# Issuing a third load ahead of the entry barrier, and a small row of the second load on another engine's queue

## The chip, the cores and the metric

One core of a Trainium2 chip. The metric is the device time of one execution in microseconds (us). The profile of an execution is shorter by about 1.3 us, since its span runs from the first to the last instruction. A run is called slow when it is over 1.5% above the fastest of the same kernel; verdicts and ratios use fast runs alone.

## The reference

```python
def reference(x):                      # x: (16, 1024, 512) float32
    x_scaled = x / 2.0
    x_max = np.max(x_scaled, axis=-1, keepdims=True)
    exp_x = np.exp(x_scaled - x_max)
    return exp_x / np.sum(exp_x, axis=-1, keepdims=True)
```

It is a softmax over the last axis: 16384 rows of 512 numbers, 33.55 MB in and as much out.

## The kernel before

The rows are loaded in ten tiles of 3, 5, 15, 15, ... rows per partition. ScalarE takes the exponential of each row and its sum, VectorE the reciprocals and the products, SyncE issues the stores. Loads 0 and 1 are issued ahead of the barrier with which the program starts; GpSimd issues the last two loads, which reuse space. (The maximum is not subtracted unless the row sums fall out of range; that path is not taken here.)

```python
TILES = [(3, 0), (5, 3), (15, 8), (15, 23), ...]      # rows per partition, place in the arena
SPREAD = 1

def load(eng, t):
    r = tiles[t][1]
    parts = [(0, P, 0, r)]
    if t == SPREAD:      # second load: four rows, then its last row on 126 and on 2 partitions
        parts = [(0, P, 0, r - 1), (0, 126, r - 1, r), (126, P, r - 1, r)]
    for p, q, lo, hi in parts:
        eng.dma_start(out=sb(t)[p:q, lo:hi], in_=dram(xf, t)[p:q, lo:hi]).then_inc(ld[t], 16)

def early():                      # put in ahead of the entry barrier
    load(nc.sync, 0)
    load(nc.scalar, 1)

def loads():                      # behind it
    for t in range(2, min(LATE)):
        load(nc.scalar, t)
# ... cut: for t in range(len(tiles)): TensorE waits for ld[t] and lets ScalarE go on;
#     GpSimd waits for s_exp >= starts.index(TURN), TURN = 83 rows, and for the stores whose
#     space loads 8 and 9 reuse, and then issues these
```

## Time and profile before

| | |
|---|---|
| time | 159.91 us (159.89 to 159.91) |
| span of the profile | 158.7 us |
| DMA | 423 GB/s over the span |
| ScalarE, VectorE busy | 51%, 46% |
| last multiply ends, last store lands | 143.6 us, 158.7 us |

How to read it: no engine is busy for much more than half of the span, while the 16 DMA engines are full. What sets the end is how fast 67.11 MB go through them, and the last store only waits for its turn. The lines are in the prediction below. There and below, an issuing engine's ring is the list of packets that its transfers have waiting on one DMA engine.

### The profile page before, as it was taken

The numbers are of one execution on the slowest core, as the hardware profiler recorded it, in microseconds if no ns is written. First come the engines' busy times: TensorE is split into PE (matmuls) and PEld (weight loads), VectorE is DVE, ScalarE is ACT, GpSimd is POOL, SyncE is SP. The second block draws the span as 40 slices with busy tenths as digits, with TensorE's granted clock in tenths as the row PEclk, the third lists the DMA queues.
The fourth block names the chain that finished last, engine by engine and source line by source line (L and its number), as shares of the span: only waits on it lengthen the run. The fifth ranks groups of instructions, "written<-read, shape, count | busy, mean of one in ns | idle before, by whom it ended". The sixth has DMA issues, their size and how long they took to land. (4 is left out here: it accounts for less than half of the span.)

```text
span 158.7 us, 657 instructions
## 1 busy us (share of the span) xinstructions
PE 0.2 (0%) x2; PEld 0.1 (0%) x2; DVE 73.2 (46%) x27; ACT 80.8 (51%) x257; POOL 2.2 (1%) x8
## 2 busy tenths in 40 slices
PE   0000000000000000000000000000000000000000
PEld 0000000000000000000000000000000000000000
DVE  0047001992981990059500991008932981992000
ACT  0590598697498008940399001991597009940000
POOL 0000000000000000000000300000000000010000
DMA  7999998989999999999999999999999999999995
GB/s 271 382 496 396 463 437 324 480 382 485 410 457 410 457 410 449 418 449 418 441 426 441 426 434 434 426 441 426 441 418 449 418 449 410 457 403 465 403 457 256
DMA packets 3024, 67.11 MB, mean 423 GB/s; under 512 B 336, under 2 KB 336, under 8 KB 720
## 3 DMA queue, kind: packets, MB, share of 16 engines
q1 hardware_dynamic: 1584, 34.34, 50.4%
q10 hardware_dynamic: 1152, 24.90, 37.1%
q0 software_dynamic: 288, 7.86, 11.5%
HBM read 33.55 MB, written 33.55 MB: 423 GB/s over the span
## 5 line engine op out<-in xcount | busy, mean ns | idle before, releaser
L271 ACT ACTIVATE arena<-arena x125 | 76.8, 615 | 54.1 <-ACTq L140 54.1
L169 DVE TENSOR_TENSOR arena<-arena,recip 128x7680 f32<-128x7680 f32 (+2 forms) x12 | 70.2, 5847 | 0.4
L166 DVE RECIPROCAL recip<-stats 128x15 f32<-128x15 f32 (+2 forms) x12 | 2.7, 224 | 70.4 <-ACT arena L271 61.4
L271 ACT ACTIVATION_READ_ACCUMULATOR arena<-arena x125 | 23.4, 187 | 0.0
L200 ACT ACT_TABLE_LOAD x1 | 1.3, 1283 | 5.7 <-issue 5.7
L119 POOL DMA_DIRECT2D arena<-in_x_dram x2 | 1.3, 638 | 84.9 <-ACT arena L271 84.9
L204 ACT ACTIVATE arena<-arena 128x512 f32<-128x512 f32 x3 | 1.9, 619 | 0.0
L180 POOL TENSOR_SCALAR inside<-stats 128x128 f32<-128x128 f32 x1 | 0.6, 630 | 51.7 <-ACT arena L271 51.7
L204 ACT ACTIVATION_READ_ACCUMULATOR arena<-arena 128x1 f32 x3 | 0.6, 188 | 0.0
L196 PE MATMUL total<-ones,count 128*1 128x1 f32 x2 | 0.2, 164 | 143.9 <-DVE inside L184 143.9
L184 DVE SCALAR_TENSOR_TENSOR inside<-inside,stats 128x128 f32<-128x128 f32 x1 | 0.3, 282 | 0.0
L188 DVE TENSOR_SCALAR flag<-total 1x1 int32<-1x1 f32 x1 | 0.1, 146 | 0.3 <-PE total L196 0.3
L196 PEld LDWEIGHTS total<-ones,count 128*1 128x1 f32 x2 | 0.1, 80 | 143.9 <-DVE inside L184 143.9
L175 POOL MEMSET ones<- 128x1 f32 x1 | 0.1, 98 | 2.2 <-POOLq L37 2.2
L306 POOL MEMSET const-bfloat16-1.0<- 128x1 bf16 x1 | 0.1, 108 | 0.0
L306 POOL MEMSET const-uint8-127<- 128x1 uint8 x1 | 0.1, 108 | 0.0
L306 POOL MEMSET const-float32-0.0<- 128x1 f32 x1 | 0.1, 104 | 0.2 <-issue 0.2
L306 POOL MEMSET const-float32-1.0<- 128x1 f32 x1 | 0.1, 104 | 0.0
L184 DVE DVE_READ_ACCUMULATOR inside<-inside,stats 128x1 f32 x1 | 0.1, 80 | 0.0
## 6 DMA issues: line engine op xcount, KB each, us to landing
out_dram<-arena SPq DMA_DIRECT2D x8, 3840.0 KB, 26.2
arena<-in_x_dram ACTq DMA_DIRECT2D x6, 3840.0 KB, 46.7
arena<-in_x_dram POOLq DMA_DIRECT2D x2, 3840.0 KB, 33.6
out_dram<-arena SPq DMA_DIRECT2D x1, 1280.0 KB, 22.9
arena<-in_x_dram ACTq DMA_DIRECT2D x1, 1024.0 KB
arena<-in_x_dram SPq DMA_DIRECT2D x1, 768.0 KB, 5.6
out_dram<-arena SPq DMA_DIRECT2D x1, 768.0 KB, 14.6
arena<-in_x_dram ACTq DMA_DIRECT2D x1, 252.0 KB
```

The costliest lines, as they stand in the source:

```text
L119: eng.dma_start(out=sb(t)[p:q, lo:hi], in_=dram(xf, t)[p:q, lo:hi]).then_inc(ld[t], 16)
L166: nc.vector.reciprocal(out=recip[:, b : b + c], in_=stats[:, b : b + c])._wait_ge(s_exp, ks[-1] + 1).then_inc(s_rec, 1)
L169: nc.vector.tensor_mul(out=arena[:, a : a + c], in0=arena[:, a : a + c], in1=recip[:, b : b + c].unsqueeze(2).to_broadcast([P, c, D]),)._w ...
L175: nc.gpsimd.memset(ones[:, :], 1.0).then_inc(s_ones, 1)
L180: nc.gpsimd.tensor_scalar(out=inside[:, :], in0=stats[:, :], scalar1=LO, scalar2=HI, op0=Alu.max, op1=Alu.min,)._wait_ge(s_exp, len(sizes) ...
L184: nc.vector.scalar_tensor_tensor(out=inside[:, :], in0=inside[:, :], scalar=1.0, in1=stats[:, :], op0=Alu.mult, op1=Alu.is_equal, accum_ou ...
L188: nc.vector.tensor_scalar(out=flag[:, :], in0=total[:, :], scalar1=float(N), scalar2=None, op0=Alu.is_ge,)._wait_ge(s_tot, 1).then_inc(s_f ...
L196: nc.tensor.matmul(total[:, :], lhsT=count[:, :], rhs=ones[:, :], start=True, stop=True)._wait_ge(s_cnt, 2).then_inc(s_tot, 1)
L200: nc.scalar.preload_act_table(Exp)
L204: ins = nc.scalar.activation(out=arena[:, b], in_=arena[:, b], func=Exp, scale=0.5, accum_out=stats[:, b : b + 1],)
L271: ins = nc.scalar.activation(out=data, in_=data, func=Exp, scale=0.5, accum_out=stats[:, r : n_rows - E + 1 + r][:, bass.ds(now, 1)],)
L306: nc = _bacc.Bacc("TRN2", target_bir_lowering=False, num_devices=1)
```

## The change

Its intent is to have the third load in the queue sooner, to free ScalarE of two issues at the start, and to let the small row of the second load travel on a second queue.

```diff
-            eng.dma_start(
+            (eng if q - p == P else nc.sync).dma_start(
                 out=sb(t)[p:q, lo:hi], in_=dram(xf, t)[p:q, lo:hi]
             ).then_inc(ld[t], 16)
 ...
         load(nc.scalar, 1)
+        load(nc.scalar, 2)
 ...
-        for t in range(2, min(LATE)):
+        for t in range(3, min(LATE)):
             load(nc.scalar, t)
```

> **What bounds the kernel now.** I read the page first (busy shares, slices, chain), then the DMA view, then windows along the span, then the timeline of the first 20 us, where the change lies.
>
> ```profile
> span 158.7 us, 657 instructions
> ...
> PE 0.2 (0%) x2; PEld 0.1 (0%) x2; DVE 73.2 (46%) x27; ACT 80.8 (51%) x257; POOL 2.2 (1%) x8
> ...
> DMA  7999998989999999999999999999999999999995
> GB/s 271 382 496 396 463 437 324 480 382 485 410 457 410 457 410 449 418 449 418 441 426 441 426 434 434 426 441 426 441 418 449 418 449 410 457 403 465 403 457 256
> DMA packets 3024, 67.11 MB, mean 423 GB/s; under 512 B 336, under 2 KB 336, under 8 KB 720
> ```
>
> No engine is busy for more than 51% of the span, while the 16 DMA engines stand at 8 or 9 tenths in every slice but the first and the last. 67.11 MB must move (33.55 in, 33.55 out), so the bound is the transfer of bytes. The chain of waits ends at 144.3 us, 14 us before the span does, and carries only 6% of it: the rest of the end is a store in flight, which the chain does not show.
>
> ```profile
> 134.67 2.83 DVE arena L169
> ...
> 140.81 2.83 DVE arena L169
> 143.63 0.22 DVE inside L184 x2
> ...
> 144.12 0.15 DVE flag L188
> ```
>
> The last store is issued when the multiply of 140.81 ends (143.64). The semaphore updates in the trace say that the store before it lands at 148.7 to 149.6 us, so the last store stands in the ring some 5 us before its turn. That 5 us is the slack of compute at the end. The packet records give the sum: 2048 packets of 30720 bytes take 1.138 us each (2330.6 us), 256 of 6144 bytes 0.234 (59.9), 128 of 8192 bytes 0.309 (39.6), 128 of 2048 bytes 0.084 (10.8), 128 of 10240 bytes 0.385 (49.3): 2490.2 us of engine time, over 16 engines 155.6 us. First data moves at 1.0 us, last at 158.18, that is 157.2 us. So only 1.5 us in the whole kernel is not packets at their usual pace, and a change of the issue order has to get its gain out of this 1.5 us.
>
> Where it lies, by packets that took longer than usual, as a mean over 16 engines: 0.25 us in the first load's first packets, 0.13 in the second load's, 0.37 in the first packet of the third load on every engine (1.5 instead of 1.14 us, all starting 6.4 to 7.0), 0.39 around 24 to 27 us where the first store gives way to the second. The start in the timeline:
>
> ```profile
> 0.00 0.38 SPq L119 DMA_DIRECT2D arena<-in_x_dram  x1
> 0.13 5.51 ACTq L119 DMA_DIRECT2D arena<-in_x_dram  x9
> ...
> 5.67 1.28 ACT L200 ACT_TABLE_LOAD   x1 [5.67 <-issue]
> 6.96 0.63 ACT L204 ACTIVATE arena<-arena 128x512 f32<-128x512 f32 x1
> ...
> 8.82 0.61 ACT L271 ACTIVATE arena<-arena  x1
> ...
> 10.94 4.48 SPq L137 DMA_DIRECT2D out_dram<-arena  x2
> ...
> 17.71 0.63 ACT L271 ACTIVATE arena<-arena  x1 [5.73 <-ACTq L140]
> ```
>
> ScalarE issues nine loads in 5.51 us, loads its table, works the first load from 6.96, the second (five rows) from 8.82 and then waits for the third until 17.71. The single instructions: second load 0.13 to 0.52, its 126-partition part 0.56 to 1.22, the 2-partition part 1.25 to 1.49, the barrier, then the third load at 2.66. Yet the third load's first packet moves at 6.45, 3.4 us after its issue ended, because the rings are full of the first two loads until then.
>
> ```profile
> 1.00:2.00 1.00, 0.00 (x0) 0.00 (x0) 0.00 (x0) 0.00 (x0) 0.00 (x0) 1.00 0.92 283
> 2.00:3.00 1.00, 0.00 (x0) 0.00 (x0) 0.00 (x0) 0.00 (x0) 0.10 (x1) 1.00 0.96 391
> 3.00:4.00 1.00, 0.00 (x0) 0.00 (x0) 0.00 (x0) 0.00 (x0) 0.00 (x0) 1.00 0.98 401
> 4.00:5.00 1.00, 0.00 (x0) 0.00 (x0) 0.00 (x0) 0.00 (x0) 0.00 (x0) 1.00 1.11 449
> ```
>
> The last two columns are DMA share and GB/s: from 2 us on the engines are full (0.96 and more). The barrier, which holds the third load until 2.66, starves nothing.
>
> **What the Trainium skill says.** "DMA: Bandwidth & Descriptors", section "Issuing engines are not separate DMA queues": transfers from ScalarE and SyncE run on the same 16 engines, and issuing from several saves only the sequencer's issue time. The trace agrees: 423 GB/s over everything. Same page, "Queues, rings and completion order": the two issuers own one ring each on every engine, and the engine goes round robin between rings packet by packet. The trace agrees: the first store, 768 KB, which alone would need 1.9 us (128 x 0.234 / 16), takes 14.6 us to landing, because its eight packets per engine alternate with 30 KB packets of the loads (starts about 1.37 us apart, and 1.138 + 0.234 is 1.372). Same page, "Why a DMA increments its semaphore by 16 and not by 1": the number of engines is the largest divisor up to 16 of the slowest dimension, so the 126-partition part runs on 14 engines (9 packets each) and the 2-partition part on 2 (the lowest numbered); the packet records carry no engine, so the trace shows this at most by its 0.67 us issue, longest of the nine.
>
> **The change part by part.** Bytes, packets and the engines they run on stay the same; two things move.
>
> (a) The third load's issue (0.36 us) comes ahead of the barrier, from 2.66 to about 0.56 on ScalarE. It is in the ring some 2 us earlier, but the ring has older work until 6 us: worth 0 by itself.
>
> (b) The two small parts (0.67 + 0.24 us of issue) go from ScalarE to SyncE. ScalarE is through its early issues at about 0.13 + 0.39 + 0.04 + 0.36 = 0.92 instead of 1.49; SyncE at 0.38 + 0.04 + 0.67 + 0.03 + 0.24 = 1.36 instead of 0.38. The barrier waits for the later of the two, so it falls some 0.1 to 0.2 us earlier. Behind it five loads of about 0.52 us remain: 2.5 + 2.6 = 5.1 instead of 5.64. The table load starts near 5.15, the first activation near 6.45 instead of 6.96, the first store is issued near 10.4 instead of 10.94. All of it beside a full DMA: 0 at the end.
>
> (c) The order on the rings changes, and this is the largest effect to be seen. The small row's 2 KB packets now stand on SyncE's ring behind the first load, beside ScalarE's ring of second and third load. When the first load ends (4.3 to 4.9 us), half of the second load is out (of 8 packets per engine some 4 are left). Alternating, SyncE's ring gives its completion and four small packets for ScalarE's four remaining 8 KB packets and completion. From there each small packet waits behind a 30 KB packet of the third load. Five are left and a completion: on engines with nine, 6.3 + 0.37 + 6 x 1.14 + 5 x 0.08 = 13.9 us; on the two engines that also have the tenth, two rounds more, 16.3. Before, the second load was known complete at 7.9 us. So it lands at 14 to 17 us, 6 to 9 later.
>
> (d) What this delays: ScalarE's five rows of the second load run from about 16.5 to 19.6 (5 x 0.615), the third load's fifteen (9.23 us) from 19.6 to 28.9 instead of 17.71 to 27.05. The fourth load lands at 28.9 in either kernel (activation at 29.26), so ScalarE has caught up there. VectorE's multiply of the second load ends near 19.7 + 0.2 + 2.83 = 22.8, its store is issued there instead of 15.09. But in the kernel before that store stood in the ring until 25.9 us, behind the first store. The first store now starts behind the small row, near 14, and needs 8 x 1.37 = 11 us, so until 25: the second store is still in time or nearly. The third store goes from 35.5 to about 37.4; loads take the turns left free.
>
> Sum on the path that sets the end: bytes 0, issue 0, idle DMA 0, and from the 1.5 us of slow packets a piece that may change: 0.37 us for the third load's first packet and 0.39 at the hand-over between stores. I take -0.1 for both together.
>
> **The rivals.**
> 1. Gain of the full 0.37 us: with the third load in the ring early, its first read is hidden under the mixed packets. For it: 30 KB packets that alternate with 6 KB stores show no such excess. Against it: the third load had been in the ring for 3.4 us before it started slow, so a late issue was not the cause. It would make 159.5.
> 2. The late second load carries on: late stores, late reuse of buffers, a starved DMA later. For it: compute is in order, and the second load comes before the third on ScalarE and VectorE. Against it: ScalarE has 1.5 to 11 us of waits ahead of every later load, the loads that reuse buffers are issued at 87.7 while the first three stores have landed at 57.3 already, and 5 us of slack remain at the end. If it did go through whole, it would be 160.5 to 162.
> 3. The small row does not get caught: its packets are through before the third load's start, because the ring favours SyncE. Then the second load lands near 7.5, everything runs 0.5 us earlier, and the end is the same, 159.8 to 159.9.
> 4. Small packets between 30 KB reads slow the reads: 128 packets, each with 0.3 us more on one engine, would be 2.4 us over the 16; the pairs of 6 and 8 KB show about 0.02 us more per packet, which is 0.2 us at most. It would make 160.1.
>
> **Range and chances.** Base 159.91, three runs within 0.02, less 0.1: 159.8. Rival 1 gives the low side, 159.3 with some gain at the store hand-over; rivals 2 and 4 the high side, 160.3. Over 2% is 3.2 us: for faster, twice the 1.5 us there is, so 0.01; for slower, 3 us of newly idle DMA, which only rival 2 in a shape I can't see would bring: 0.02.
>
> **What would show it.** Right: the second load's first activation at 14 to 17 us instead of 8.82 and the table load near 5.15 (steps b, c); ScalarE without a wait between second and third load, and at the fourth load back to about 29.3 (d); second store issued near 23; DMA at 9 tenths throughout and a last store still issued 3 us or more before its predecessor lands. Wrong: a slice with the DMA under 8 tenths between 10 and 150 us (rival 2), the second load complete before 9 us (rival 3), 30 KB packets over 1.3 us while small ones remain (rival 4), or the end moved by more than 0.5 us with none of these.

## The result and the profile after

The changed kernel takes 160.97 us (160.4 to 161.65, six runs), the kernel before in the same rounds 159.92 (159.89 to 160.07). The ratio is 1.0059, with a 95% interval of 1.0032 to 1.0086. A ratio here is the mean time of one kernel's fast runs over that of the other's fast runs of the same rounds, so it is not quite the ratio of the medians. The change is "within 2%", as foreseen, but it costs some 0.6%, the runs scatter over 1.2 us where those of before scatter over 0.2, and 160.97 lies outside the predicted range.

The page after, the rows that answer to those of before (busy times; DMA share and GB/s in 40 slices):

```profile
span 159.6 us, 657 instructions
...
PE 0.2 (0%) x2; PEld 0.1 (0%) x2; DVE 73.2 (46%) x27; ACT 80.5 (50%) x257; POOL 2.2 (1%) x8
...
DMA  7999999999899999999999999999999989898986
GB/s 277 465 391 401 450 425 375 444 467 436 377 485 393 470 393 470 416 446 408 439 446 416 400 423 393 470 400 470 393 470 393 477 385 477 385 485 385 477 385 262
DMA packets 3024, 67.11 MB, mean 420 GB/s; under 512 B 336, under 2 KB 336, under 8 KB 720
```

Work, packets and bytes are the same; only the mean rate has fallen, from 423 to 420 GB/s, with the DMA engines as full as before. So nothing starves: the same packets take longer.

The timeline of the start, after (start, length, engine, line, operation; in brackets the idle time before it):

```profile
0.00 1.17 SPq L119 DMA_DIRECT2D arena<-in_x_dram  x3
0.12 4.63 ACTq L119 DMA_DIRECT2D arena<-in_x_dram  x7
...
4.78 1.28 ACT L201 ACT_TABLE_LOAD   x1 [4.78 <-issue]
6.08 0.63 ACT L205 ACTIVATE arena<-arena 128x512 f32<-128x512 f32 x1
...
10.05 28.22 SPq L137 DMA_DIRECT2D out_dram<-arena  x3
17.09 0.63 ACT L272 ACTIVATE arena<-arena  x1 [9.07 <-ACTq L140]
...
20.51 2.82 DVE L170 TENSOR_TENSOR arena<-arena,recip 128x2560 f32<-128x2560 f32 x1
...
29.76 8.16 DVE L170 TENSOR_TENSOR arena<-arena,recip 128x7680 f32<-128x7680 f32 x1
```

ScalarE's issues end 0.9 us earlier, and the first load is worked on 0.9 us earlier (6.08, before 6.96). The second load's work starts at 17.09 where it started at 8.82; from there on ScalarE runs without a wait through the third load. All this is as foreseen. The chain that ended last:

```profile
138.39 2.82 DVE arena L170
141.21 0.22 DVE inside L185 x2
...
141.71 0.15 DVE flag L189
```

The last multiply ends at 141.21, 2.4 us *earlier* than before (143.63), and still the last store lands later: its sixteen completions come at 157.73 to 158.66 before and at 158.23 to 159.59 after, four of the latter behind 159.1. Compute has gained and the DMA has lost.

Windows of the two kernels show where (start:end, length, busy time of five engines, clock, DMA share, GB/s). Before:

```profile
20.00:60.00 40.00, 0.00 (x0) 0.00 (x0) 25.23 (x6) 25.71 (x85) 0.00 (x0) 1.00 1.00 426
60.00:100.00 40.00, 0.00 (x0) 0.00 (x0) 16.82 (x4) 20.03 (x65) 1.27 (x2) 1.00 1.01 435
100.00:150.00 50.00, 0.19 (x2) 0.09 (x2) 26.22 (x13) 26.43 (x86) 0.63 (x1) 1.00 1.00 433
```

After:

```profile
20.00:60.00 40.00, 0.00 (x0) 0.00 (x0) 28.24 (x8) 30.24 (x99) 0.00 (x0) 1.00 1.00 431
60.00:100.00 40.00, 0.00 (x0) 0.00 (x0) 16.82 (x4) 18.76 (x63) 1.27 (x2) 1.00 0.99 420
100.00:150.00 50.00, 0.19 (x2) 0.09 (x2) 26.22 (x13) 25.38 (x83) 0.63 (x1) 1.00 1.00 433
```

Between 60 and 100 us the rate is 420 GB/s instead of 435, at a DMA share of 0.99 (between 20 and 60 us it is a little higher than before, 431 instead of 426). Nothing in the source points at that stretch: the change is in the first 3 us.

For the rest I use the trace's packet records. Each packet has a usual duration by its size (30720 bytes 1.138 us, 8192 bytes 0.309, 6144 bytes 0.234, 2048 bytes 0.084); "excess" is what the packets took beyond it, summed and divided by the 16 engines. Excess by the time at which packets start, in us:

| profile of | 0-20 | 20-40 | 40-100 | from 100 | sum | last store lands: first, median, last engine | run's time |
|---|---|---|---|---|---|---|---|
| before | 0.86 | 0.39 | 0.01 | 0.07 | 1.33 | 157.7, 158.0, 158.7 | 160.05 |
| after | 1.00 | 0.12 | 0.81 | 0.02 | 1.95 | 158.2, 158.5, 159.6 | 160.98 |

The mean engine loses 0.62 us more, and the slowest engine 0.93 us more.

### The profile page after: what moved, and what is told of

Its sections match the earlier page's. It is cut to its first block, busy times and chain, and to the rows that moved or that the text cites. A ratio compares the mean times of both kernels' runs of the same rounds, so it can differ in the third digit from the quotient of the medians.

```text
span 159.6 us, 657 instructions
## 1 busy us (share of the span) xinstructions
PE 0.2 (0%) x2; PEld 0.1 (0%) x2; DVE 73.2 (46%) x27; ACT 80.5 (50%) x257; POOL 2.2 (1%) x8
```

## The experiments

Theories at the start: **A**, the order on the rings costs the time (2 KB packets of the small row alternate with 30 KB packets of the third load, and the second load is late because of it); **B**, the early issue of the third load itself does. All sixteen experiments gave correct results. The kernel before ran beside every job, 44 times in all. Ten of those were slow (166.8 to 168.7 us), so slow runs belong to no variant in particular; the fast ones lay between 159.75 and 160.13. e1 to e4 are one job; f1, its reference, f4 and f5 the next; then g1 to g4 and h1 to h4.

**e1: the third load early, the small row left on ScalarE.** From the changed kernel:

```diff
-            (eng if q - p == P else nc.sync).dma_start(
+            eng.dma_start(
```

> Only the third load's early issue; the small row stays on ScalarE's ring, ahead of the third load. Theory A (the order on the rings costs the time: small packets alternating with the third load's 30 KB packets, and the second load late because of it): packets come in the order of the kernel before, so 159.9 +- 0.2 us, second load complete near 7.9 us. Theory B (the early issue of the third load itself costs): 160.4 to 161.6.

Measured: 159.94 us, ratio 0.9999 (0.9986 to 1.0013), second load complete at 7.91. B falls: the early issue is worth nothing and costs nothing.

**e2: the small row on SyncE, the third load behind the barrier.** From the changed kernel: `load(nc.scalar, 2)` taken out of `early()` and put back into `loads()`.

> Only the small row on SyncE's ring; the third load issued behind the barrier, near 2.3 us, still before the rings reach it at 6.3. Theory A: as the changed kernel, 160.4 to 161.6 us with scatter over 0.5, second load complete near 16.7. Theory B: 159.9 +- 0.2.

Measured: 160.69 us (160.48 to 161.02), ratio 1.0053 (1.0040 to 1.0066), second load complete at 16.89. This half of the change carries all of its cost.

**e3: the small row issued ahead of the first load.**

```diff
-        load(nc.sync, 0)
         load(nc.scalar, 1)
+        load(nc.sync, 0)
         load(nc.scalar, 2)
```

> The changed kernel with the small row issued ahead of the first load on SyncE, so that it alternates with 8 KB packets and is through before the third load starts. Theory A: second load complete near 8 us, 159.9 +- 0.3 us, small scatter. Theory B, or SyncE's issue of a 14-engine transfer as the cost: 160.4 to 161.6.

Measured: four of seven runs slow (164.0 to 164.5); the fast ones 159.95, 160.19 and 160.28, ratio 1.0020 (1.0002 to 1.0039). The design was poor: with the small row in front, it was now the first load that met the third, and its completions came at 14.2 to 16.8 us instead of 5.6. Under A the cost should have moved, not vanished; the run tells little.

**e4: the second load's work late, the loads' packets as before.** From the kernel before:

```diff
         for t in range(len(tiles)):
+            if t == SPREAD:
+                nc.tensor.wait_ge(ld[t + 1], 16)
             nc.tensor.wait_ge(ld[t], 48 if t == SPREAD else 16).then_inc(...)
```

> The kernel before, in which the work on the second load is held until the third has landed (near 17 us); the loads' packets unchanged. Splits theory A: A1 (lateness of the second load's work and of the stores behind it, which shifts how stores and loads meet on the engines later) 160.4 to 161.6 us with scatter; A2 (small packets among 30 KB packets and the engines put out of step by them) 159.9 +- 0.2.

Measured: 159.90 us (159.80 to 160.04), ratio 1.0001 (0.9989 to 1.0014). The lateness was reproduced:

```profile
17.68 0.63 ACT L273 ACTIVATE arena<-arena  x1 [8.69 <-PEq L196]
...
21.11 2.82 DVE L169 TENSOR_TENSOR arena<-arena,recip 128x2560 f32<-128x2560 f32 x1
```

ScalarE takes up the second load at 17.68 and VectorE multiplies it at 21.11, both even later than in the changed kernel, and the kernel is no slower. So A1 falls as it stood: the late second load and the late second and third store, by themselves, cost no time. A2, the packets themselves, remains, and so does a mixture of both: e4's trace does have late slow reads, 0.36 us per engine between 40 and 100 us, though no small packet is out of place (see below the table of profiles).

**f1 and its reference: the small row even over all engines**, as one 128-partition transfer, once on SyncE (from the changed kernel), once on ScalarE (from the kernel before):

```diff
-            parts = [(0, P, 0, r - 1), (0, 126, r - 1, r), (126, P, r - 1, r)]
+            parts = [(0, P, 0, r - 1), (0, P, r - 1, r)]
```

> The changed kernel with the small row as one 128-partition transfer on SyncE's ring: eight 2 KB packets on every engine. Theory S (2 KB packets among 30 KB packets slow those, on any engine): 0.4 to 0.7 us over its own reference, the same even row on ScalarE's ring. Theory O (the uneven split puts the 16 engines out of step: nine packets on 12 of them, ten on two, none on two): within 0.2 us of its reference.

> The kernel before with the small row as one 128-partition transfer on ScalarE's ring: the reference of the run above. Two engines carry 16 KB more than before each (some 0.6 us of packets) and two 4 KB less, so 160.0 to 160.6 us under either theory.

Measured: on SyncE 160.50 to 162.82 in five fast runs, ratio to the kernel before 1.0078 (1.0037 to 1.0118); the reference fell into the slow state in five of six runs, its one fast run took 160.75. The even row is about as slow on either ring, as far as one run can say, and whatever sets that time covers the effect looked for. Inconclusive.

**f5 and f4: one of the two parts on SyncE.** From the changed kernel, `nc.sync if q - p == 2 else eng` for f5, `nc.sync if q - p == 126 else eng` for f4. f4 ran in three jobs, because most of its runs were slow.

> The changed kernel with only the 2-partition part on SyncE's ring; the 126-partition part stays on ScalarE's ring ahead of the third load. Theory S: two small packets in all, 159.9 +- 0.15. Theory O, if the two engines with an extra packet on that ring are what is out of step: 160.2 or more.

> The changed kernel with only the 126-partition part on SyncE's ring; the 2-partition part stays on ScalarE's ring, behind the second load. Theory S: the whole cost, 160.4 us or more. Theory O, if the two engines with a tenth packet are what is out of step: 159.9 to 160.1; if the two engines with none are: 160.4 or more.

> The run with only the 126-partition part on SyncE's ring again, since most of its runs fell into the slow state: 160.4 to 161.2 us in the fast ones, if the nine small packets on 14 engines carry the cost; 159.9 to 160.1 if the tenth packet on two engines does.

> Only the 126-partition part on SyncE's ring, a third time. If it carries the cost: fast runs 160.4 to 161.0. If the cost needs the 2-partition part as well: 159.9 to 160.1. With most runs in the slow state it stays open.

Measured: f5 has three fast runs of six, 159.91, 159.97 and 160.31, ratio 1.0013 (0.9999 to 1.0028): the 2-partition part alone costs little or nothing. f4 has one fast run in each job, 160.85, 159.95 and 160.45, 15 of 18 being slow. Two of three speak for the 126-partition part as the carrier; it stays unsettled. All three profiles kept of f4 are of slow runs. For what they are worth, they show the early slow reads of the changed kernel (0.15 to 0.17 us per engine between 7 and 10 us) but hardly any late ones (0.03 or less between 40 and 100 us; their slow packets there are stores).

**g2: part of the small row on SyncE, but no 2 KB packet beside a 30 KB packet.** 56 of the 126 partitions (four packets on each of 14 engines) stay on SyncE, and 70 (five packets) go back to ScalarE's ring. By the order on the rings, four small packets go out while the second load's 8 KB packets last. From the changed kernel:

```diff
-            parts = [(0, P, 0, r - 1), (0, 126, r - 1, r), (126, P, r - 1, r)]
+            parts = [(0, P, 0, r - 1), (0, 56, r - 1, r), (56, 126, r - 1, r), (126, P, r - 1, r)]
 ...
-            (eng if q - p == P else nc.sync).dma_start(
+            (nc.sync if q - p == 56 else eng).dma_start(
```

> The changed kernel with 56 of the small row's partitions (four packets on each of the 14 engines) on SyncE's ring, and the other 70 (five packets each) and the 2 on ScalarE's ring ahead of the third load. SyncE's small packets are through while the second load's 8 KB packets last, so no small packet meets a 30 KB packet; queues, engines and bytes else as in the changed kernel. Theory S: second load complete near 8 us, 159.9 +- 0.2 us. If a 14-engine transfer on SyncE's ring, or the barrier and issue times, cost: 160.4 or more.

Measured: four of eight runs slow; the four fast ones 159.79 to 159.94, ratio 1.0002 (0.9987 to 1.0018); second load complete at 8.2. The cost is gone. Four small packets on SyncE, on 14 engines, with a third load issued early, cost nothing when they are through before the 30 KB packets start. But g2 takes away more than the meeting of small and large packets: the second load is no longer late, so the second store is in time too, and no engine has a tenth packet on SyncE's ring. It does not tell these apart. (The 2-partition part is on ScalarE here too; f5 says that it matters little by itself.)

**g1: twice as many small packets**, each half as large. From the changed kernel, the 126-partition part is cut into columns 0 to 255 and 256 to 511:

```diff
-            parts = [..., (0, 126, r - 1, r), ...]
+            parts = [..., (0, 126, r - 1, r, 0, D // 2), (0, 126, r - 1, r, D // 2, D), ...]
```

> The changed kernel with the 126-partition part cut into two halves of 1 KB rows, both on SyncE's ring: 18 small packets per engine instead of nine, the same bytes. Theory S (small packets alternating with 30 KB loads, and what that sets off): the slowed 30 KB reads (1.24 instead of 1.14 us) last from 7 to some 23 us instead of 13, the second load lands near 24, and the time is 161 to 162.5 us. If instead the alternation costs nothing and only the chance of slow reads at 57 to 93 us counts: 160.4 to 161.0 as the changed kernel.

Measured: 160.33 us (160.01 to 160.83), ratio 1.0033 (1.0015 to 1.0051), second load complete at 25.9. A miss for theory S in its simple form: with twice as many encounters the cost is smaller. The packet records show less to pay: beside 1 KB packets the 30 KB reads take 1.14 us, later 1.15 to 1.17 (excess 0.003 us per engine between 7 and 10 us, 0.2 in the changed kernel). So it is not the number of small packets. Yet g1 has late slow reads too, 0.45 us per engine, with almost no early ones.

**g3: the changed kernel again**, for a second trace.

> The changed kernel again, for a second trace: 160.4 to 161.6 us. If slow 30 KB reads between 57 and 93 us belong to the changed order, their sum over the mean engine is 0.5 us or more here too (0.81 in the first trace, 0.01 in the kernel before); if they came by chance into one trace, near 0.

Measured: 160.90 us (160.54 to 161.10), ratio 1.0057 (1.0044 to 1.0071). The excess between 40 and 100 us is 0.90 us, as in the first trace (0.81), and again four engines land more than a microsecond after the median (159.6 to 159.7). The late excess belongs to the changed order; it did not come by chance into one trace.

**h1, h2, h3: is it the moment at which GpSimd's first load joins the rings?** In both traces of the changed kernel the largest cluster of slow reads lies at 88 to 94 us (0.54 to 0.60 us per engine), where GpSimd's first load joins while ScalarE's last load ends. The changed kernel issues GpSimd's loads at 85.4 us, the kernel before at 87.7. h1 (from the changed kernel) and h2 (from the kernel before) release them five rows earlier; h3 (from the changed kernel) puts fourteen small writes ahead of them:

```diff
-TURN = 83
+TURN = 78                                    # h1, h2
 ...
         nc.gpsimd.wait_ge(s_exp, starts.index(TURN))
+        for i in range(14):                  # h3
+            nc.gpsimd.memset(pad[:, 64 * i : 64 * i + 64], 0.0)
```

> The changed kernel with GpSimd's two loads released five rows earlier, so issued near 82.3 instead of 85.4 us. Theory J (the slow reads at 88 to 94 belong to GpSimd's load joining just as ScalarE's last load ends): other packets meet at the join, the slow reads of 88 to 94 shrink from 0.6 us to under 0.2, time 160.2 to 160.5. Theory E (the engines are out of step from the start, and pay wherever): slow reads of the same sum elsewhere, 160.5 to 161.2.

> The kernel before with GpSimd's two loads released five rows earlier, so issued near 84.6 instead of 87.7 us, about where the changed kernel has them (85.4). Theory J: slow reads at the join here too, 160.2 to 160.8 us. Theory E: 159.9 +- 0.15, no slow reads.

> The changed kernel with fourteen small writes of GpSimd ahead of its two loads, so that they are issued some 1 to 3 us later, near where the kernel before issues them. Theory J: under 0.2 us of slow reads at 88 to 97, time 160.2 to 160.5. Theory E: 160.5 to 161.2.

Measured: h1 161.26 us, ratio 1.0078 (1.0062 to 1.0093), issue at 82.3; h2, in its four fast runs of six, 159.76 to 159.83, ratio 0.9990 (0.9975 to 1.0005), issue at 84.6; h3 160.86 us, ratio 1.0050 (1.0028 to 1.0072), issue at 86.2, only 0.8 us later than without the writes. (The record's verdict for each of the three is "unclear"; five of the job's eleven runs of the kernel before were slow.) The kernel before has no slow read at an earlier join, and the changed kernel stays slower wherever the join comes. One reading fits J: in h3's profile, which is of its fastest run, the slow reads of 88 to 97 us are 0.13 us. But e2's loads join at 85.5 us, as the changed kernel's do, and its profile has 0.13 us there and 0.53 between 57 and 88. Theory J falls as an explanation of the cost. Theory E, something that the changed order carries along from the start, is left, though h1 is a little over its range (161.2); that the engines are out of step is its picture, which no run isolates.

The rate between 60 and 100 us in the profiles of the variants (windows as above): e1, f5 and h2 first, each of which sends the nine small packets ahead of the third load:

```profile
60.00:100.00 40.00, 0.00 (x0) 0.00 (x0) 16.82 (x4) 20.00 (x65) 1.27 (x2) 1.00 1.01 434
```

```profile
60.00:100.00 40.00, 0.00 (x0) 0.00 (x0) 16.82 (x4) 19.99 (x65) 1.27 (x2) 1.00 1.01 436
```

```profile
60.00:100.00 40.00, 0.00 (x0) 0.00 (x0) 16.82 (x4) 18.86 (x61) 1.27 (x2) 1.00 1.01 434
```

Then e2, g3 and h1, in which they alternate with it:

```profile
60.00:100.00 40.00, 0.00 (x0) 0.00 (x0) 16.82 (x4) 19.28 (x64) 1.27 (x2) 1.00 1.00 426
```

```profile
60.00:100.00 40.00, 0.00 (x0) 0.00 (x0) 16.82 (x4) 18.58 (x61) 1.27 (x2) 1.00 1.00 422
```

```profile
60.00:100.00 40.00, 0.00 (x0) 0.00 (x0) 16.82 (x4) 17.67 (x59) 1.27 (x2) 1.00 1.00 422
```

434 to 436 GB/s in the first group, 422 to 426 in the second, at a DMA share of 1.01 and 1.00. The three other profiles of fast runs lie between: h3 429, g1 430, e4 431. The same as excess, for every profile of a fast run, in the order of the profiled run's time:

| profile of | excess 0-20 | 20-40 | 40-100 | sum | last engine lands | time |
|---|---|---|---|---|---|---|
| h2 (before, join earlier) | 0.88 | 0.28 | 0.01 | 1.19 | 158.4 | 159.77 |
| e4 (before, late work) | 0.90 | 0.00 | 0.37 | 1.29 | 158.4 | 159.80 |
| e1 (third load early only) | 0.81 | 0.28 | 0.01 | 1.13 | 158.5 | 159.89 |
| f5 (2 partitions on SyncE) | 0.79 | 0.27 | 0.01 | 1.10 | 158.5 | 159.91 |
| before | 0.86 | 0.39 | 0.01 | 1.33 | 158.7 | 160.05 |
| h3 (after, join later) | 0.90 | 0.16 | 0.43 | 1.54 | 158.7 | 160.07 |
| g1 (1 KB packets) | 0.62 | 0.34 | 0.47 | 1.45 | 158.7 | 160.14 |
| e2 (small row only) | 1.08 | 0.02 | 0.71 | 1.83 | 159.1 | 160.48 |
| after | 1.00 | 0.12 | 0.81 | 1.95 | 159.6 | 160.98 |
| g3 (after again) | 1.17 | 0.01 | 0.90 | 2.10 | 159.7 | 161.10 |
| h1 (after, join earlier) | 0.91 | 0.10 | 0.99 | 2.02 | 160.0 | 161.41 |

The time goes with the slow packets of 40 to 100 us. h3's profile is of its fastest run, 160.07, where its other five took 160.59 to 161.10: the same kernel with half the late excess loses little. e4 shows that 0.37 us there can be made up by what is missing at 20 to 40.

Most of what these excesses stand for are 30 KB reads of the loads, not stores. Packets of one engine, from the packet records (start + duration; the ring by its issuer: A ScalarE, S SyncE, G GpSimd; all 30 KB but those marked):

```
before, 6-11 us  6.45+1.50A  7.95+1.15A  9.09+1.14A  10.23+1.14A
after,  6-11 us  6.08+1.14A  7.21+0.08S(2KB)  7.29+1.24A  8.53+0.09S(2KB)  8.61+1.23A  9.84+0.09S(2KB)  9.93+1.24A
after,  an engine without small packets
                 6.49+1.14A  7.62+1.22A  8.84+1.23A  10.06+1.23A
before, 90-96 us 90.58+1.14S  91.72+1.14A  92.85+1.14G  93.99+1.14A  95.12+1.14G
after,  90-96 us 90.63+1.39A  92.02+1.43G  93.44+1.14S  94.58+1.14G
after,  one of three engines that are a packet out of step there
                 88.89+1.43A  90.31+1.15G  91.46+1.14S  92.59+1.95A  94.53+1.14G
```

In the first row the third load's first packet takes 1.50 us and the rest 1.14. In the second the first packet is no longer slow, but each of the following ones takes 1.22 to 1.30, on engines that carry small packets and on the two that carry none. That is some 0.5 us per engine between 7 and 14 us, for the 0.37 that was saved. In the last two rows reads of two loads follow each other and take up to 1.95 us; in the kernel before (fourth row) four reads in a row take 1.14 each.

One more thing in the packet records goes with the late slow reads: when the second store gets going. In the two kernels a store for which SyncE's ring has run empty sends its first packet 3.7 to 3.9 us after its issue (before: stores 1 and 3; after: stores 1, 2 and 3). Before, the second store was issued at 15.09, long in time, and its packets follow the first store's. After, it is issued at 23.37, the first store is through by some 25 us on most engines, and the ring gives nothing until 27.18.

| | second store issued | its first packet | it lands | third store lands | slow reads 40-100, us per engine |
|---|---|---|---|---|---|
| before | 15.09 | 25.9 | 37.4 to 38.0 | 56.6 to 57.3 | 0.00 |
| after | 23.37 | 27.2 | 38.6 to 40.0 | 59.0 to 59.5 | 0.77 |
| e4 (no small packet out of place) | 23.96 | 28.1 | 39.6 to 40.1 | 60.1 to 62.0 | 0.36 |

All 18 profiles fall in two groups. Where the second store's first packet moves at 24.7 to 25.9 us (before, e1, f5, h2, g2, the three of f4, f1 and its reference) the late reads have an excess of 0.03 us or less; where it moves at 27.1 us or later (after, g3, e2, h1, h3, e4, g1, e3) it is 0.16 to 0.95. (Seven of the 18 are of slow runs: e3, g2, f4, f1 and its reference. Their slow packets are mostly stores, but they are no firm ground.) So the late slow reads go with a late second store, with or without 2 KB packets beside 30 KB packets. That it sets them off is not shown; and by itself it does not cost time, since e4 is as fast as the kernel before.

## Why the prediction was wrong

By its own steps:

- **The bound, and that issue and barrier are worth nothing (a, b): right.** e1 shows it for the early third load. The sizes of (b) were a little low: the part over 126 partitions took 0.45 us to issue on SyncE, not the 0.67 of ScalarE, so the third and later loads were ahead by more, and the table load came at 4.78 rather than 5.15.
- **The order on the rings (c): right.** Foreseen was the second load complete at 13.9 us on engines with nine small packets and at 16.3 on the two with ten; fourteen semaphore updates came at 14.3 to 14.9 and two at 16.7, which also bears out the split over 14 and 2 engines.
- **What that delays (d): the times of issue right, "the second store is still in time or nearly" wrong by a turn.** Second store issued at 23.4 (foreseen 22.8), third at 37.9 (37.4), ScalarE without a wait until the fourth load, DMA full throughout, slack at the end larger. But the second store's first packet moves 3.8 us after its issue, at 27.2 instead of 25.9, and this store and the third land 1.2 to 2.4 us later than before. The kernel before shows the same time, and the prediction read it otherwise: of the first store's 14.6 us to landing, which it put down to the alternation of packets, 3.9 pass before its first packet (10.94 to 14.86). Rival 2, late work that leaves the DMA idle later, did not come: the DMA stays full, and e4, with the same lateness alone, gives 1.0001.
- **The sum, which took "-0.1 for both together" out of the 1.5 us of slow packets: this is the step that failed.** The two pieces named did shrink: the third load's slow first packet (0.37 us) is gone, as rival 1 had it, and the hand-over of the stores fell from 0.39 to 0.12. But the step treated every other packet as having a fixed duration, and that does not hold. The 30 KB reads beside 2 KB packets took about 0.1 us more each on all sixteen engines; rival 4 had sized this at 0.02 per packet and 0.2 us in all, from the pairs of 6 and 8 KB packets, and it is 0.5. And 0.8 to 0.9 us of slow packets, nearly all of them reads, appeared between 40 and 100 us, which no rival had. The sum of slow packets went from 1.33 to 1.95 us instead of to 1.2.
- **The end as the mean engine: a second miss in the same sum.** The last store is complete when its slowest engine is. After the change the median engine lands 0.5 us later, the last one 0.9 us later. Whether this also makes the scatter (the changed kernel's runs lie 0.5 to 1.7 us above the median of before) is not shown, since only profiled runs have packet records.
- **The range**, 159.3 to 160.3, followed from a spread of 0.5 us about a quantity that the working had no measured bound for on the slow side. The signs named for "wrong" were partly there: 30 KB packets of up to 1.31 us while small ones remained. The late reads were not.

What is shown: the cost comes from the small row's place on SyncE's ring (e2), not from the early issue (e1), not from the late second load alone (e4), not from the moment at which GpSimd's load joins (h1, h2, h3), and it is absent when the small packets are through before the 30 KB packets start (g2), which also puts the second store back in time. The traces show it as slow reads, most of them 40 us and more after the small packets are gone, and as engines that end apart. What stays open is why reads are slow then, and which consequence of the small row's place brings it: the 2 KB packets beside 30 KB packets, the second store that starts a turn late, or the two engines with a tenth packet, on which the first store lands at 27.7 us and on the others by 25.8. f1 was to test the last and was inconclusive. That the ring order sets which reads and writes meet on the engines for the rest of the run, and that some meetings are slow, fits the lines above, but no run isolates it. Nor is it explained why 1 KB packets nearly leave the reads alone where 2 KB packets do not (g1), nor settled whether the 126-partition part alone would do (f4).

No variant beat the kernel before clearly: h2, at 0.9990 (0.9975 to 1.0005), is the best of them.

## What to carry to other kernels

In this kernel, bound by full DMA engines, an earlier issue was worth nothing (e1), but moving a transfer to another issuer's queue changed the order of packets for the whole run and cost 0.5% (e2); it was a change of order, not of issue cost. Ask of such a change what the moved packets will stand beside, and what is delayed behind them; the variant in which the small packets passed before the large ones came, and the next store stayed in time, cost nothing (g2). And take the end from the slowest of the 16 engines: here the mean engine lost 0.62 us and the slowest 0.93, so a sum of packet durations divided by 16 hid a third of the loss.

## What the Trainium skill lacked or had wrong

- "DMA: Bandwidth & Descriptors", section "Issuing engines are not separate DMA queues": it says that issuing from several engines saves only issue time. It does not say that it can cost: the small row moved to SyncE's queue makes the kernel 0.53% slower (e2), with the same bytes on the same DMA engines.
- Same page, "Queues, rings and completion order": the round robin between rings holds packet by packet (second load complete at 14.3 to 14.9 us on engines with nine packets and 16.7 with ten). Not stated: a transfer's completion, a packet of 4 bytes in the trace, takes a turn of its own. In the kernel before, the first store's last data packets start at 23.4 us, its completion comes in the next turn at 24.7, and the second store's first data only at 25.9, though it had been in the ring since 15.4.
- Same page, section "Bandwidth": no page that I read has it that the duration of one and the same packet depends on its neighbours. A 30 KB read took 1.14 us in most of the run, 1.22 to 1.30 while 2 KB packets of another ring alternated with reads (on engines without such packets too), 1.14 to 1.17 beside 1 KB packets, and up to 1.95 where two loads met.
- No page that I read has the slow state of a single core: runs of 164 to 169 us at a granted clock of 1.00, the kernel before in 10 of 44 runs. In the profiles of such runs stores on one to seven of the 16 DMA engines take up to 1.8 us per 30 KB packet instead of 1.14 in a stretch between some 47 and 97 us (in e3 57 to 118), and those engines land the last store 4 to 8 us after the others. Its frequency differed between variants (15 of 18 runs of f4, none of 17 of the changed kernel and e2); this was not followed up and plays no part in the verdicts.
